# A two-layer trunk with eight experts on one core: the long-list path moved ahead, gate and up tiles side by side, the last group and the norm in a written order

## The chip, the core and the metric

One NeuronCore of a Trainium2 chip runs one program. It has TensorE (PE, matmuls, with its weight loads as PEld), VectorE (DVE), ScalarE (ACT), GpSimd (POOL) and SyncE (SP, which here issues nearly all DMAs). The metric is the device time of one execution in microseconds; "before" is the median of three runs, and one more execution was profiled.

## The reference

```python
for l in range(DEPTH):                      # 2 layers, 256 tokens, width 1024
    h = rms_norm(x, norm_mix[l])
    x = x + hybrid_mixer(h, ...)
    h = rms_norm(x, norm_ffn[l])
    if l % 2 == 0: x = x + swiglu(h, ...)       # dense, 3584 hidden units
    else:          x = x + moe_swiglu(h, ...)   # top 2 of 8 experts, 3584 hidden units each
return rms_norm(x, norm_final)

def swiglu(x, wg, wu, wd):
    return (jax.nn.silu(x @ wg) * (x @ wu)) @ wd
```

All weights are f32 in HBM, some 426 MB, of which the experts are 352 MB. Each is read once.

## The kernel before

The weights come as one stream of tiles of 128x2048 f32 (1 MB), in the order of use. An expert has 14 groups of 256 hidden units; a group has three tiles: gate (`ig`), up (`iu`) and down (`idn`). The eight experts are 112 groups, counted here from 0 to 111; the last expert has groups 98 to 111. I write idn(104) for the down tile of group 104.

A matmul takes f16. Each tile is therefore split into a high half, which ACT writes (the *head*, L113: scale and round), and a low half, which DVE writes (the *tail*, L117: what is left). Only the down tile of every odd group stays f32 and goes to PE whole (`whole`). So an even group has three tiles to split and an odd group two, 280 in all.

An expert works on the up to 80 tokens of its list (`CAP`). `gate_up(n)` is 96 matmuls (L287 to L289: high by high, high by low, low by high), first the gate tile's 48, then the up tile's 48; L289 is the one that needs the tail. Then ACT takes Silu of the gate half (L803), DVE multiplies by the up half (L807), and in even groups ACT and DVE split the product (L811, L812). `down(n)` adds the product with the down tile to two accumulators (L718 split, 12 matmuls; L712 whole, 8 instructions); it stands behind `gate_up(n+1)` on PE, so that the hidden step is covered. After the 14 groups of an expert the accumulators are copied (`evacuate`: L726, L727) and scattered back to the rows (`combine`: L736, L738).

In this stage the order on PE, DVE and ACT is the order in which the code is written (`manual_schedule`). `groups()` writes for each group n: gate_up(n), down(n-1), and then a loop of k heads and tails, with Silu behind the first head, the product behind the first tail, and L811 and L812 behind the second pair. k comes from `lead`, the number of tiles that shall be split ahead: it falls from 7 to 3 over the 112 groups. Loads go through SP; a tile's buffer is one of eleven, and SP issues a load when a buffer is free and the eighth load before it has landed.

Behind the last `gate_up` and before the last `down` stands a path for lists longer than 80 tokens (L837): if a count exceeds 80, a loop computes the rest with all tokens. With these inputs no list is that long, and each engine only branches past it. Behind it stand the last down, the last combine, the final norm (squares on ACT with a sum per half row, L930; sums, root and reciprocal per block of 128 rows, L931 to L934; scaling, L938 to L945) and four output DMAs (L946). That part is ordered by the scheduler.

Of the kernel before, what the change touches and what calls it, by code (L numbers as in the profile page):

```python
# [14 lines left out]
P = 128  # L15
T = 256
# [22 lines left out]
LEAD = (7.0, 3.0)  # L39

# [15 lines left out]
def trunk(ctx: ExitStack, tc: tile.TileContext, x, w, small, gates, last, out):  # L56
# [62 lines left out]
    def split_tile(i, r):  # L119

        t = spl.tile([P, 2, 2048], F16, name="hl")
# [301 lines left out]
    def gate_up(ig, iu, h, n, between=None):  # L423
# [80 lines left out]
    def moe(l, accs, extra_load):  # L504
# [226 lines left out]
        def combine(e, ye, c=None):  # L731
            for c in range(2) if c is None else (c,):
                for q in range(2):
                    o = mm((P, half))
                    for part in range(2):
                        PE.matmul(o, sgt[e][:, c * P:(c + 1) * P], ye[:, part, q * half:(q + 1) * half],  # L736
                                  start=(part == 0), stop=(part == 1))
                    V.scalar_tensor_tensor(yts(c, q), o.rearrange("p (n t) -> p n t", n=2), comb[:, c, e:e + 1],  # L738
                                           yts(c, q), op0=OP.mult, op1=OP.add)
# [31 lines left out]
        def groups():  # L771
            ready = None
            for n, (e, g) in enumerate(steps):
# [20 lines left out]
                lead = LEAD[0] + (LEAD[1] - LEAD[0]) * n / (len(steps) - 1)  # L794
                k = max(1 if n == 0 else 0, used + int(lead) - todo["n"])
# [3 lines left out]
                for j in range(k + 2):  # L799
# [29 lines left out]
            return before  # L829

        counts = {}
        with tc.manual_schedule(engines={mybir.EngineType.PE, mybir.EngineType.DVE, mybir.EngineType.Activation}):
            routing()
            before = groups()
        longest = counts["longest"]

        with tc.If(longest > CAP):  # L837
# [11 lines left out]
            hh = lambda part, k: h[:, part, k]  # L849
            for e in range(NE):  # L850
# [158 lines left out]
```

## Time and profile before

| | us |
|---|---|
| median of three runs | 1252.37 (1252.36 to 1254.17) |
| the profiled execution | 1254.29 |
| its span, first to last instruction | 1252.5 |
| PE busy | 1170.6 (93%) |
| DVE busy | 995.7 (79%) |
| ACT busy | 825.3 (66%) |

[...] The loads moved 343 GB/s over the whole span and about 419 GB/s over its second half, up to the last 40 us. A row of the timeline names start, duration, engine, line, operation and count, and in brackets how long the engine had been idle and what released it.

### The profile page before, as it was taken

How to read it: one execution, taken by the hardware profiler on the slowest of the kernel's cores; microseconds unless marked ns; L12 is line 12 of the kernel's file. 1: busy time of each engine (PE TensorE's matmuls, PEld its weight loads, DVE VectorE, ACT ScalarE, POOL GpSimd, SP SyncE). 2: the span in 40 equal slices, each digit the busy share in tenths (PEclk: the TensorE clock that was granted, in tenths of full speed). 3: DMA queues.
4: the chain of work that ended last, by engine and by line, in shares of the span. 5: the costliest groups of instructions: out<-in, count | busy, mean ns of one | idle time of the engine just before them, and what ended most of it. 6: DMA issues, size and time to landing. Idle time of an engine off the chain costs nothing. (4 is left out here: it accounts for less than half of the span.)

```text
span 1252.5 us, 34703 instructions
## 1 busy us (share of the span) xinstructions
PE 1170.6 (93%) x15707; PEld 902.4 (72%) x15707; DVE 995.7 (79%) x915; ACT 825.3 (66%) x814; POOL 0.8 (0%) x7
## 2 busy tenths in 40 slices
PE   6999999999999989999999898998989899899985
PEld 5887888888888766776676666766657676666663
DVE  7798666666888787998888797888789788779875
ACT  6965444444685686777767676766666676766764
POOL 0000000000000000000000000000000000000000
PEclk9999999999999999999999999999989999999998
DMA  9976555555547789999999999999999999999991
GB/s 360 420 292 241 203 202 202 202 203 202 194 161 285 265 312 396 420 420 419 418 420 419 420 419 420 419 419 419 419 420 417 419 419 417 420 418 413 419 366 69
DMA packets 61358, 431.84 MB, mean 345 GB/s; under 512 B 6928, under 2 KB 7056, under 8 KB 10000
## 3 DMA queue, kind: packets, MB, share of 16 engines
q1 hardware_dynamic: 61200, 429.52, 85.3%
q8 instruction: 125, 2.05, 0.7%
q14 instruction: 33, 0.27, 0.1%
HBM read 428.44 MB, written 1.05 MB: 343 GB/s over the span
## 5 line engine op out<-in xcount | busy, mean ns | idle before, releaser
L117 DVE SCALAR_TENSOR_TENSOR hl<-raw,hl 128x2048 f16<-128x2048 f32 x269 | 611.0, 2281 | 123.5 <-ACT hl L113 122.0
L113 ACT ACTIVATE hl<-raw 128x2048 f16<-128x2048 f32 x269 | 508.9, 1901 | 158.4 <-DMA raw<-in_w 156.6
L288 PEld LDWEIGHTS <-hl 128*128 128x128 f16 x4704 | 468.2, 100 | 39.2 <-issue 19.7
L289 PEld LDWEIGHTS <-hl 128*128 128x128 f16 x4704 | 467.6, 99 | 39.3 <-DVE hl L117 20.5
L287 PEld LDWEIGHTS <-hl 128*128 128x128 f16 x4704 | 468.1, 100 | 36.5 <-issue 14.9
L289 PE MATMUL mm<-he,hl 128*128 128x80 f16 x3584 | 398.6, 202 | 16.3 <-DVE hl L117 16.0
L287 PE MATMUL mm<-he,hl 128*128 128x80 f16 x3584 | 399.1, 202 | 0.0
L288 PE MATMUL mm<-he,hl 128*128 128x80 f16 x3584 | 399.0, 202 | 0.0
L125 DVE SCALAR_TENSOR_TENSOR hl<-raw,hl 128x2048 f16<-128x2048 f32 (+1 forms) x78 | 176.0, 2260 | 72.1 <-ACT hl L124 71.9
L287 PE MATMUL mm<-h,hl 128*128 128x256 f16 x768 | 209.0, 273 | 3.0 <-ACT h L237 2.8
L288 PE MATMUL mm<-h,hl 128*128 128x256 f16 x768 | 209.5, 273 | 1.8 <-DVE h L238 1.6
L289 PE MATMUL mm<-h,hl 128*128 128x256 f16 x768 | 209.5, 273 | 1.6 <-DVE hl L125 1.6
L712 PE MATMUL acc<-raw,hdm 128*80 128x512 f32 x448 | 210.3, 614 | 0.0
L124 ACT ACTIVATE hl<-raw 128x2048 f16<-128x2048 f32 (+1 forms) x78 | 146.1, 1881 | 93.3 <-PE mm L289 86.2
L718 PE MATMUL acc<-hl,hdm 128*80 128x512 f16 x672 | 161.9, 389 | 12.2 <-DVE hdm L812 9.5
L712 PEld LDWEIGHTS acc<-raw,hdm 128*80 128x80 f32 x448 | 65.6, 155 | 100.6 <-issue 99.2
L718 PEld LDWEIGHTS <-hdm 128*80 128x80 f16 x672 | 75.8, 120 | 76.8 <-DVE hdm L812 15.2
L803 ACT ACTIVATE sg<-mm 128x160 f32<-128x160 f32 x112 | 32.9, 294 | 46.9 <-PE mm L289 46.3
L288 PE MATMUL acc<-hd,hl 128*128 128x256 f16 x224 | 60.9, 273 | 0.2 <-DVE hd L462 0.2
L289 PE MATMUL acc<-hd,hl 128*128 128x256 f16 x224 | 60.9, 273 | 0.0
L287 PE MATMUL acc<-hd,hl 128*128 128x256 f16 x224 | 60.6, 273 | 0.0
L811 ACT ACTIVATE hdm<-sg 128x160 f16<-128x160 f32 x56 | 18.6, 333 | 35.1 <-DVE sg L807 32.7
(227 smaller groups left out, 606.1 us busy)
## 6 DMA issues: line engine op xcount, KB each, us to landing
raw<-in_w SPq DMA_DIRECT2D x400, 1024.0 KB, 19.7
raw<-in_w SPq DMA_DIRECT2D x6, 512.0 KB, 15.4
xT<-in_x SPq DMA_DIRECT2D x4, 256.0 KB, 3.9
gw<-in_gates SPq DMA_DIRECT2D x2, 512.0 KB, 9.9
gw<-in_w SPq DMA_DIRECT2D x1, 512.0 KB, 6.7
r<-in_w SPq DMA_DIRECT2D x1, 512.0 KB, 3.5
ig<-in_w SPq DMA_DIRECT2D x1, 512.0 KB, 5.6
a<-in_w SPq DMA_DIRECT2D x1, 512.0 KB, 6.5
```

Source lines behind the costliest of these rows:

```text
L113: S.activation(hi, src, AF.Copy, scale=SW)
L117: V.scalar_tensor_tensor(lo, src, SW, hi, op0=OP.mult, op1=OP.subtract)
L124: S.activation(hi, src, AF.Copy, scale=SW)
L125: V.scalar_tensor_tensor(lo, src, SW, hi, op0=OP.mult, op1=OP.subtract)
L287: PE.matmul(o, wt[0][:, cols], a_hi, start=start, stop=False, skip_group_check=True)
L288: PE.matmul(o, wt[0][:, cols], a_lo, start=False, stop=False, skip_group_check=True)
L289: PE.matmul(o, wt[1][:, cols], a_hi, start=False, stop=stop, skip_group_check=True)
L712: PE.matmul(eaccs[e][q], hd[:, c], wt[c][:, q * half:(q + 1) * half], start=(g == 0 and c == 0), stop=(g == NG - 1 and c == 1), skip_group ...
L718: PE.matmul(eaccs[e][q], hd[:, part, c], wt[wpart][:, c * D + q * half:c * D + (q + 1) * half], start=(g == 0 and c == 0 and part == 0 and ...
L803: S.activation(sg, bank[:, 0], AF.Silu, scale=IN_SCALE)
L811: S.activation(hd[:, 0], hf, AF.Copy)
```

## The change

- The path for long lists now stands eight groups ahead of the end (`REST`): `groups` runs to group 103, then comes the path, then groups 104 to 110, then `last_group`. The path loads its tiles through POOL into other buffers, and its tiles share the `hl` tag.
- `CLOSE` caps the lead at 2 in the last twelve groups and at 1 in the last four; behind the hidden step of each group a new loop splits up to three tiles ahead (one in group 110).
- The experts' gate and up weights are laid side by side (`sided`): the first tile of a group holds gate and up of its first 128 units, the second those of the other 128. `gate_up` takes the first tile's products for both, then the second's.
- `last_group` writes the last group out: its two tiles are split in halves, down(110) stands between the two halves of gate_up(111), the hidden step runs per 128 units, and the last down, the last combine and the norm follow in a written order on all three engines.

```diff
+CLOSE = ((12, 2.0), (4, 1.0))
+REST = 8
...
-        n = 2 if i in (0, NT - 2, NT - 1) else 1
+        n = 2 if i in (0, NT - 3, NT - 2, NT - 1) else 1
...
-        for a in range(2):
+        sided = not (isinstance(iu, int) and iu < MOE)
+        for t in range(2):
             for k in range(KD):
-                for c in range(2):
-                    mm3(o[a][c], wts[a], slice(k * 256 + c * P, k * 256 + (c + 1) * P), h(0, k), h(1, k),
+                for n in range(2):
+                    a, c = (n, t) if sided else (t, n)
+                    mm3(o[a][c], wts[t], slice(k * 256 + n * P, k * 256 + (n + 1) * P), h(0, k), h(1, k),
                         start=(k == 0 and (a, c) in first), stop=(k == KD - 1))
-            if a == 0 and between is not None:
-                between()
+            if t == 0 and between is not None:
+                between(*banks)
...
-        def groups():
-            ready = None
-            for n, (e, g) in enumerate(steps):
+        def groups(begin, end):
+            ready, before = later["ready"], later.get("before")
+            for n, (e, g) in list(enumerate(steps))[begin:end]:
...
                 lead = LEAD[0] + (LEAD[1] - LEAD[0]) * n / (len(steps) - 1)
+                lead = min([lead] + [x for at, x in CLOSE if n >= len(steps) - at])
...
+                for j in range(used + (1 if n == len(steps) - 2 else 3) - todo["n"]):
+                    next_heads()
+                    next_tails()
...
+        def last_group():
...
+            def unit(bank, c):
+                S.activation(sg[:, c], bank[:, 0, c], AF.Silu, scale=IN_SCALE)
+                V.scalar_tensor_tensor(hd[:, c], bank[:, 1, c], IN_SCALE * SY * SW, sg[:, c], op0=OP.mult, op1=OP.mult)
+            def between(bank):
+                down(*later["before"])
+                for n, piece in enumerate(pieces[iu]):
+                    head(piece)
+                    tail(piece)
+                unit(bank, 0)
+            for piece in pieces[ig]:
+                head(piece)
+                tail(piece)
+            bank = gate_up(ig, iu, lambda part, k: he[:, k, part], CAP, between)[0]
+            unit(bank, 1)
+            ready = B("ready", 1)
+            S.activation(ready, onesf, AF.Sqrt)
...
+            def square(c, q):
+                junk = t4(("a", "th")[q], (P, half))
+                S.activation(two(junk), yts(c, q), AF.Square, accum_out=fs[:, c, q:q + 1])
+            def rms(c):
+                V.scalar_tensor_tensor(fr[:, c:c + 1], fs[:, c, 1:2], 1.0 / D, pre[:, c:c + 1], op0=OP.mult, op1=OP.add)
+                S.activation(fr[:, c:c + 1], fr[:, c:c + 1], AF.Sqrt)
...
+            for c in range(2):
+                for q in range(2):
+                    add_up(e, ye, c, q)
+                    square(c, q)
+                    if q == 0:
+                        if c == 1:
+                            rms(0)
+                        V.tensor_scalar(pre[:, c:c + 1], fs[:, c, 0:1], 1.0 / D, EPS, op0=OP.mult, op1=OP.add)
+            scaled(0, 0)
+            V.reciprocal(fr[:, 0:1], fr[:, 0:1])
+            scaled(0, 1)
+            put(0)
+            rms(1)
+            scaled(1, 0)
+            V.reciprocal(fr[:, 1:2], fr[:, 1:2])
+            scaled(1, 1)
+            put(1)
...
             routing()
-            before = groups()
+            groups(0, len(steps) - REST)
...
-                            r = rawp.tile([P, 2048], F32, name="raw")
...
-                            nc.sync.dma_start(r, w[bass.ds(at, 1)].rearrange("o p c -> (o p) c"))
-                            split_tile(("spill", n), [(slice(0, 2048), r)])
+                            r = [(slice(j * 1024, (j + 1) * 1024), t4(t, (P, 1024))) for j, t in enumerate(SPARE[0])]
+                            for sl, t in r:
+                                G.dma_start(t, w[bass.ds(at, 1)].rearrange("o p c -> (o p) c")[:, sl])
+                            split_tile(("spill", n), r, spill[n])
...
-        ready = B("ready", 1)
-        S.activation(ready, xT[:, 0, 0:1], AF.Square)
-        S.activation(ready, ready, AF.Sqrt)
-        down(*before)
-        combine(NE - 1, evacuate(NE - 1))
+        with tc.manual_schedule(engines=ordered):
+            groups(len(steps) - REST, len(steps) - 1)
+            last_group()
```

ACT's instructions behind the hidden step of group 103, before: the heads (L113) of the tiles of group 104, then Silu (L803) and product copy (L811) of group 104, Silu of 105 and Silu of 106 among the heads of the next tiles.

```order
L113 ACTIVATE hl<-raw 128x2048 x3
L803 ACTIVATE sg_18341<-mm 128x160
L113 ACTIVATE hl<-raw 128x2048
L811 ACTIVATE hdm<-sg_18342 128x160
L113 ACTIVATE hl<-raw 128x2048
L803 ACTIVATE sg_18467<-mm 128x160
L113 ACTIVATE hl<-raw 128x2048 x3
L803 ACTIVATE sg_18591<-mm 128x160
```

The same place in the change, from where the path (L937) ends; head is L117, Silu L814, copy L822.

```order
L937 UNCONDITIONAL_BRANCH
L117 ACTIVATE hl<-raw 128x2048
L814 ACTIVATE sg_19968<-mm 128x160
L822 ACTIVATE hdm<-sg_19969 128x160
L117 ACTIVATE hl<-raw 128x2048 x2
L814 ACTIVATE sg_20094<-mm 128x160
L117 ACTIVATE hl<-raw 128x2048 x3
L814 ACTIVATE sg_20219<-mm 128x160
```

In the even group 104 the copy moved ahead of the second head; in the odd group 105 the order is the same. Groups 100, 102 and 106 read alike; in 108 both heads stand behind the copy.

DVE at the change's passage of the path: tails are L121, the product L818.

```order
L818 SCALAR_TENSOR_TENSOR hdm<-mm,sg_18218 128x160
L121 SCALAR_TENSOR_TENSOR hl<-raw,hl 128x2048
L937 COMPARE_AND_BRANCH
L939 TENSOR_SCALAR over<-slot 128x16
L940 TENSOR_TENSOR over<-over,comb 128x16
L952 TENSOR_LOAD each
```

The branch now stands behind the tail of the second tile of group 104, where before it stood behind the first `ye` of the last expert.

DVE from the last copy of `ye` on, before: four add-ups (L738), then the norm.

```order
L727 SCALAR_TENSOR_TENSOR ye<-acc,ye 80x512
L738 SCALAR_TENSOR_TENSOR xT<-mm,comb,xT 128x2x256 x4
L931 TENSOR_TENSOR fr<-fs 128x1
L938 TENSOR_TENSOR uc<-xT,cs 128x512
L932 TENSOR_SCALAR fr<-fr 128x1
L938 TENSOR_TENSOR uc<-xT,cs 128x512
L934 RECIPROCAL fr<-fr 128x1
```

The same in the change: add-ups are L742, `pre` is L919.

```order
L733 SCALAR_TENSOR_TENSOR ye<-acc,ye 80x512 x2
L742 SCALAR_TENSOR_TENSOR xT<-mm,comb,xT 128x2x256
L919 TENSOR_SCALAR pre<-fs 128x1
L742 SCALAR_TENSOR_TENSOR xT<-mm,comb,xT 128x2x256 x2
L896 SCALAR_TENSOR_TENSOR fr<-fs,pre 128x1
L919 TENSOR_SCALAR pre<-fs 128x1
L742 SCALAR_TENSOR_TENSOR xT<-mm,comb,xT 128x2x256
L910 TENSOR_TENSOR uc<-xT,cs 128x512
L921 RECIPROCAL fr<-fr 128x1
```

`pre` and the first block's sum, which need ACT's squares, now stand between the add-ups.

## Rows read from the trace of the kernel before

**Rows 1.** The page: a costly group (line, form, count, busy, idle), and DMA issues.
```profile
L113 ACT ACTIVATE hl<-raw 128x2048 f16<-128x2048 f32 x269 | 508.9, 1901 | 158.4 <-DMA raw<-in_w 156.6
...
raw<-in_w SPq DMA_DIRECT2D x400, 1024.0 KB, 19.7
```

**Rows 2.** Timeline of ACT: start, duration, what, idle time before and releaser.
```profile
1174.58 1.91 ACT L113 ACTIVATE hl<-raw 128x2048 f16<-128x2048 f32 x1 [0.55 <-DMA raw<-in_w]
...
1190.99 1.91 ACT L113 ACTIVATE hl<-raw 128x2048 f16<-128x2048 f32 x1 [2.08 <-DMA raw<-in_w]
...
1208.35 1.91 ACT L113 ACTIVATE hl<-raw 128x2048 f16<-128x2048 f32 x1 [0.58 <-DMA raw<-in_w]
1210.17 0.28 ACT L803 ACTIVATE sg<-mm 128x160 f32<-128x160 f32 x1
1210.82 1.91 ACT L113 ACTIVATE hl<-raw 128x2048 f16<-128x2048 f32 x1 [0.37 <-DMA raw<-in_w]
1212.86 0.34 ACT L811 ACTIVATE hdm<-sg 128x160 f16<-128x160 f32 x1
```

**Rows 3.** Timeline of DVE, the same stretch.
```profile
1210.29 2.29 DVE L117 SCALAR_TENSOR_TENSOR hl<-raw,hl 128x2048 f16<-128x2048 f32 x1 [0.20 <-ACT hl L113]
1212.50 0.32 DVE L807 SCALAR_TENSOR_TENSOR sg<-mm,sg 128x160 f32<-128x160 f32 x1
1212.76 2.29 DVE L117 SCALAR_TENSOR_TENSOR hl<-raw,hl 128x2048 f16<-128x2048 f32 x1
```

**Rows 4.** Timeline of PE: matmuls that waited for a tail.
```profile
1124.32 0.21 PE L289 MATMUL mm<-he,hl 128*128 128x80 f16 x1 [1.94 <-DVE hl L117]
...
1215.11 0.21 PE L289 MATMUL mm<-he,hl 128*128 128x80 f16 x1 [0.35 <-DVE hl L117]
...
1222.48 0.21 PE L289 MATMUL mm<-he,hl 128*128 128x80 f16 x1 [0.56 <-DVE hl L117]
```

**Rows 5.** Stretches: length, PE, PEld, DVE, ACT, POOL busy, granted clock, DMA, GB/s.
```profile
1222.50:1237.20 14.70, 14.70 (x170) 8.76 (x170) 7.80 (x8) 5.29 (x8) 0.00 (x0) 1.00 0.14 54
1205.00:1222.50 17.50, 15.38 (x261) 11.36 (x262) 14.66 (x11) 12.42 (x10) 0.00 (x0) 1.00 0.79 315
1126.00:1127.00 1.00, 1.00 (x11) 0.76 (x10) 0.06 (x1) 1.00 (x2) 0.00 (x0) 0.50 1.02 426
1128.00:1129.00 1.00, 1.00 (x4) 0.44 (x3) 1.00 (x1) 1.00 (x1) 0.00 (x0) 0.55 0.94 385
```

**Rows 6.** Line 837, the path: queue, operation, count, ns, first and last start.
```profile
L837 SPq EVENT_SEMAPHORE  x9: 17/17/17, 1217.8 to 1228.3; - x9
...
L837 ACTq EVENT_SEMAPHORE  x2: 17/17/17, 1239.5 to 1239.6; - x2
...
L837 SPq COMPARE_BRANCH  x1: 45/45/45, 1213.7 to 1213.7; - x1
...
L837 ACTq COMPARE_BRANCH  x1: 50/50/50, 1236.4 to 1236.4; - x1
```

**Rows 7.** Timeline of all engines from the last down on.
```profile
1233.64 3.60 PE L712 MATMUL acc<-raw,hdm 128*80 128x512 f32 x8
...
1240.29 0.57 ACT L726 ACTIVATE ye<-acc 80x512 f16<-80x512 f32 x1
1240.29 2.76 PE L736 MATMUL mm<-ye,sgt 80*128 80x512 f16 x8 [3.05 <-DVEq L837]
...
1241.50 0.74 DVE L738 SCALAR_TENSOR_TENSOR xT<-mm,comb,xT 128x512 f32<-128x512 f32 x1
...
1242.28 0.62 ACT L930 ACTIVATE a<-xT 128x512 f32<-128x512 f32 x1
1242.66 2.07 DVE L738 SCALAR_TENSOR_TENSOR xT<-mm,comb,xT 128x512 f32<-128x512 f32 x3 [0.42 <-PE mm L736]
1242.81 0.19 ACT L930 ACTIVATION_READ_ACCUMULATOR a<-xT 128x1 f32 x1
...
1247.96 0.72 ACT L943 ACTIVATE ge<-ge,fr 128x512 f32<-128x512 f32 x1 [0.47 <-DVE fr L934]
```

More of the change, by code (lines that the diff above doesn't have):

```diff
@@ L729, in evacuate, with add_up, combine @@
             return ye
[L731 to L739, printed above, removed]
+        def add_up(e, ye, c, q):
+            o = mm((P, half))
+            for part in range(2):
+                PE.matmul(o, sgt[e][:, c * P:(c + 1) * P], ye[:, part, q * half:(q + 1) * half],
+                          start=(part == 0), stop=(part == 1))
+            V.scalar_tensor_tensor(yts(c, q), o.rearrange("p (n t) -> p n t", n=2), comb[:, c, e:e + 1],
+                                   yts(c, q), op0=OP.mult, op1=OP.add)
+        def combine(e, ye, c):
+            for q in range(2):
+                add_up(e, ye, c, q)
         todo = {"heads": MOE + 10, "tails": MOE + 10, "n": 9}
@@ L828, in groups, with put, scaled @@
                 before = (e, g, idn, hd)
-            return before
+            later["ready"], later["before"] = ready, before
+        def last_group():
+            e, g = steps[-1]
+            ig, iu, idn = take(3)
+            he = hes[e]
+            pieces = {}
+            for i in (ig, iu):
+                t = spl.tile([P, 2, 2048], F16, name="hl")
+                pieces[i] = list(split_pieces(raw.pop(i), t))
+                parts[i] = [t[:, 0], t[:, 1]]
+            parts[idn] = [t[:, k:k + D] for _, t in raw.pop(idn) for k in range(0, t.shape[1], D)]
+            hd = wk.tile([P, 2, CAP], F32, name="hdl", tag="xs", bufs=2)
+            sg = wk.tile([P, 2, CAP], F32, name="sg0", tag="ssq")
+            def unit(bank, c):
[14 more added lines that the diff above has]
+            S.activation(ready, onesf, AF.Sqrt)
+            wt = parts.pop(idn)
+            for c in range(2):
+                for q in range(2):
+                    PE.matmul(eaccs[e][q], hd[:, c], wt[c][:, q * half:(q + 1) * half], start=False, stop=(c == 1),
+                              skip_group_check=True)
+            ye = evacuate(e)
+            gl = late["gl"]
+            fs, pre = B("fs", 2, 2), B("pre", 2)
+            fr = B("fr", 2)
+            two = lambda t: t.rearrange("p (n t) -> p n t", n=2)
+            ots = [t4(("uc", "ge")[c], (P, D)) for c in range(2)]
+            def square(c, q):
[4 more added lines that the diff above has]
+                S.activation(fr[:, c:c + 1], fr[:, c:c + 1], AF.Sqrt)
+            def put(c):
+                for q in range(2):
+                    sl = slice(q * half, (q + 1) * half)
+                    if q == 0:
+                        S.activation(ots[c][:, sl], ots[c][:, sl], AF.Copy, scale=fr[:, c:c + 1])
+                    else:
+                        V.tensor_scalar(ots[c][:, sl], ots[c][:, sl], fr[:, c:c + 1], None, op0=OP.mult)
+                    nc.sync.dma_start(out[c * P:(c + 1) * P, sl], ots[c][:, sl])
+            def scaled(c, q):
+                sl = slice(q * half, (q + 1) * half)
+                V.tensor_tensor(two(ots[c][:, sl]), yts(c, q), two(gl[:, sl]), op=OP.mult)
+            for c in range(2):
+                for q in range(2):
+                    add_up(e, ye, c, q)
+                    square(c, q)
+                    if q == 0:
+                        if c == 1:
[10 more added lines that the diff above has]
+            put(1)
@@ L831, in moe @@
         counts = {}
-        with tc.manual_schedule(engines={mybir.EngineType.PE, mybir.EngineType.DVE, mybir.EngineType.Activation}):
+        ordered = {mybir.EngineType.PE, mybir.EngineType.DVE, mybir.EngineType.Activation}
+        with tc.manual_schedule(engines=ordered):
             routing()
-            before = groups()
+            groups(0, len(steps) - REST)
         longest = counts["longest"]
@@ L849, in moe @@
             hh = lambda part, k: h[:, part, k]
+            spill = [spl.tile([P, 2, 2048], F16, name="spill", tag="hl") for _ in range(3)]
             for e in range(NE):
@@ L918, in trunk @@
     gw[1] = gate_weights(1)
[L919 removed]
+    accs = ffn(0, h, sums, lambda *_: finish1(), later1)
     h, sums, finish = residual(accs, nm[:, 8:16])
     accs = mixer(1, h, sums, finish, lambda sd: None)
[L922 to L946 removed]
+    moe(1, accs, gl_load)
 def _stream(np, inputs):
```

45 lines of the change are left out of this document (12 added, 33 removed).

## The prediction

> **What bounds the kernel now.** I read the timeline of ScalarE (ACT), VectorE (DVE) and TensorE (PE) over the last ten groups first, then PE's busy share by stretch, then the rows of the path for long lists, then the closing timeline.
>
> [rows 1]: ACT's heads (the f16 high halves, 1.9 us each) make ACT wait 158.4 us over the run, 156.6 of it for a transfer: the experts' stage runs at the pace of the loads. [rows 2] show that pace near the end: heads that wait for their tile begin 2.47 us apart (1208.35, 1210.82). [rows 3]: DVE's tail (the low half) starts when its head ends and takes 2.29 us, so a tile is usable some 4.2 us after landing. [rows 4]: PE waits 0.35 to 0.56 us in the middle of gate_up for the tail of the up tile. For groups 108 and 109 that is a loop with little to spare: PE is busy 15.38 of 17.5 us [rows 5].
>
> From 1222.5 us on PE has no gap until 1237.2 [rows 5]: half of gate_up(110), down(109), gate_up(111), down(110), down(111). So the end of down(111), which I call E (1237.2 before), is set by when gate_up(110) gets the tail of its second tile, and anything that makes PE late there reaches the end one for one. Behind E stand the path's branch and the norm: span end 1252.5, so E + 15.3.
>
> **The branch leaves the end: gain.** In [rows 7] PE begins the combine at 1240.29 after 3.05 us of waiting for DVE's passage of the path, and the second copy of `ye` starts on ACT at the same time. Without the branch that copy begins as soon as its matmuls end, about E; the first add-up follows 1.21 us behind it as in the rows (1240.29, 1241.50), so at E + 1.25 and not E + 4.26. Gain 3.0 us.
>
> **The branch at group 104: loss.** [rows 6]: ACT's compare-and-branch is issued at 1236.4 and its next instruction runs at 1239.5, 3.1 us later; SP's takes 4.1 us (1213.7 to 1217.8) with loads still in flight. In the change the ACT branch stands behind the head of idn(104), which began at 1174.58 in the trace [rows 2]. PE's first instruction after the path waits for ACT and DVE, so gate_up(104) starts at 1174.6 + 1.1 (how late that head starts in the new order, below) + 3.1 to 4.1, about 1179 to 1180; PE is free for it at about 1176. PE's spare time until the end takes most of this back. Laid out row by row with the durations of [rows 2 to 4], 0.8 us (branch of 3.1) to 1.8 us (4.1) is left at E. I take 1.8, since SP's row is the one taken with loads in flight. PE's idle time there is 2.9 to 3.9 us. [...]
>
> The SP queue has some 20 loads behind the branch. A load lands 19.7 us after its issue [rows 1], eight tiles deep, so a pause of 4.1 us leaves the queues filled: nothing. The end of the path holds SP until its own DMA semaphores have landed (up to 1228.3 in [rows 6], where nothing stood behind it); the change moves the path's loads to POOL, and SP's row in its order keeps no such wait. If that were wrong, a pause of 14.6 us (1213.7 to 1228.3) would cost several us.
>
> [...]
>
> **The order in the last twelve groups: loss.** CLOSE does not shorten what is split ahead: the new loop behind the hidden step brings the splits back to three tiles ahead in the same group. What it changes is which instruction stands first. In every even group (100 to 108) ACT before ran head(gate of n+1), Silu, head(up of n+1), then the copy L811; now the copy (L822) stands ahead of head(up). That copy waits for DVE's L818, and L818 stands behind the tail of gate(n+1). In the rows of group 108: head at 1208.35, landing of the up tile and its head at 1210.82, tail until 1212.58, L807 until 1212.82, copy at 1212.86 [rows 2, 3]. In the new order the head of the up tile starts after the copy, at 1213.2 and not 1210.82; its tail runs 1215.1 to 1217.4 and not to 1215.05; PE's wait in the middle of gate_up(109) grows from 0.35 to 2.6 us, or to 2.2 where PE itself comes later. So +2.3 us for the odd group.
>
> It then passes into the even group: Silu(109) waits for gate_up(109) and stands ahead of head(up 110). With gate_up(109) done at 1219.2, that head begins at 1219.6 and not at its landing, 1218.2 (three tiles of 2.47 behind 1210.82); +1.3 us. PE's spare time takes back about as much as comes on, not all of it. Continuing the same steps (each op at the latest of its landing, its input and the op ahead in its queue) the second half of gate_up is late by 2.2, 1.1, 2.9, 1.8, 3.5, 2.4 us in groups 101 to 106, and, behind a pause of the loads that moved all landings from 1190.99 on by 1.4 us [rows 2], by 2.7, 1.7, 3.3, 2.2 in 107 to 110. For before the same timetable gives E within 0.2 us of the trace. Loss at E +2.2; bounds 0, if PE's slack took all of it, and +4.
>
> **Last group, side by side.** The same 96 matmuls and the same down; down(110) moves between the halves, and the half of the hidden units waits under the first half of down(111). PE has no gap to close there, so the order gains nothing: +0.1. The matmuls of all other groups are the same in number and form; only columns change place in the tile.
>
> **The norm.** Before, four add-ups ran one behind the other on DVE, 0.67 us apart, and the sums came last. Now `pre` stands on DVE behind the first add-up and waits for ACT's square of it: 0.62 + 0.19 us with hand-overs [rows 7], 0.8 us of idle DVE. The same comes again behind the third add-up, where ACT still has the second's square ahead, and the sum of the first row block waits 0.2: +1.9 with the small steps. Against that the first block's sum and root no longer stand behind the last add-up (-0.5), and the 0.42 us that DVE waited for PE behind the first add-up goes with the branch (-0.4). From the first add-up to the end of the last scaling it was 7.2 us (1241.50 to 1247.96 + 0.72), now 8.2: +1.0, bounds -0.9 (all squares hidden) and +1.5.
>
> **Sum.** 1252.5 - 3.0 (branch out of the end) + 1.8 + 1.2 (branch at group 104, clock behind it) + 2.2 (order) + 0.1 (last group) + 1.0 (norm) = 1255.8 us of span; E = 1242.5, and 13.3 behind it. The profiled execution took 1254.29 with a span of 1252.5, and the median is 1252.37, 0.13 below that span. Forecast 1255.7 us, 0.27% above before.
>
> **Rivals.** *Faster.* PE's spare time, 12% of the stretch in [rows 5], swallows both the late up tiles and the branch before group 110, so E stays at 1237.2, and the squares are hidden: 1237.2 + 12.3 - 0.9 = 1248.6 of span, 1248.5 us; it stays under the border as long as the norm costs less than +0.5. It decides at the second half of gate_up(110): it must start by 1222.5, as in [rows 4]. For it: each group has some 1 us of PE waits to give. Against: ACT's own queue, not PE, carries the delay from group to group. 0.18.
>
> *No difference.* The branch costs the moved place next to nothing (3.1 us or less, and no fall of the clock): E = 1239.5 to 1240.3, span 1252.8 to 1253.6, 1252.7 to 1253.5 us. 0.28. [...]
>
> *Slower still.* [...] 0.14.
>
> [...]
>
> **How the numbers follow.** Forecast 0.40 (own range 1254.0 to 1257.2), no difference 0.28, slower still 0.14, faster 0.18. A measurement of this kernel tells about 0.2%, 2.5 us, from no change, so 1249.9 and 1254.9 are the borders: of the forecast's 0.40 some 0.28 lies above 1254.9. Slower 0.42, same 0.40, faster 0.18. The range leaves out two thirds of the faster case and the top of the slowest: 1249.4 to 1258.8.
>
> **What would show it.** ACT's L822 ahead of the second head in even groups, with that head some 2 us after its landing; PE waits of about 2 us for L121 in the middle of gate_up(101), (103), (107); a gap of 3 to 4 us at gate_up(104) with the clock at 0.50 after it; down(111) ending at 1241 to 1244; two waits of DVE's L919 of 0.8 us; from E to the end 13.3 us. The forecast is wrong if the up heads start at their landing, if E comes before 1239, or if E to the end is under 12.5.

## The result, and the profile after

The changed kernel took 1262.67 us (median of 6 runs, 1261.53 to 1263.56) beside 1252.96 for the kernel before on the same chip: 1.0076 of before, 95% interval 1.0066 to 1.0086, so 9.7 us slower. The forecast was 1255.7 in a range to 1258.8. The direction came out, the size did not. The profiled execution took 1263.56 us with a span of 1261.5 and is the one read here.

Executions differ in where the last twelve groups begin (down(99) ends at 1151.3 to 1156.2 us in the profiles that are read below). So I count from one fixed point: the end of down(99), the down ahead of the first reordered group. These are the rows of PE's timeline (start, duration, operation) for that down and for the last one, down(111), of the kernel after:

```profile
1149.68 3.60 PE L718 MATMUL acc<-raw,hdm 128*80 128x512 f32 x8
...
1244.58 3.63 PE L881 MATMUL acc<-raw,hdl 128*80 128x512 f32 x8
```

From 1153.28 to E = 1248.21 it is 94.9 us. In the kernel before, down(99) ended at 1153.72 (the row below) and E stood at 1237.24 [rows 7]: 83.5 us.

```profile
1150.12 3.60 PE L712 MATMUL acc<-raw,hdm 128*80 128x512 f32 x8
```

So 11.4 us were lost in twelve groups; the forecast had 5.3. Behind E it is 13.3 us to the end of the span, as forecast.

**The order.** The forecast had a copy on ACT ahead of the second head. ACT's timeline of group 102 after, then that of DVE (the idle time before each operation and its releaser in brackets):

```profile
1164.84 1.90 ACT L117 ACTIVATE hl<-raw 128x2048 f16<-128x2048 f32 x1
1167.38 0.30 ACT L814 ACTIVATE sg<-mm 128x160 f32<-128x160 f32 x1 [0.64 <-PE mm L293]
1170.14 0.34 ACT L822 ACTIVATE hdm<-sg 128x160 f16<-128x160 f32 x1 [2.46 <-DVE sg L818]
1170.38 1.89 ACT L117 ACTIVATE hl<-raw 128x2048 f16<-128x2048 f32 x1
```

```profile
1163.17 6.70 DVE L121 SCALAR_TENSOR_TENSOR hl<-raw,hl 128x2048 f16<-128x2048 f32 x3 [1.47 <-ACT hl L117]
1169.79 0.32 DVE L818 SCALAR_TENSOR_TENSOR sg<-mm,sg 128x160 f32<-128x160 f32 x1
1170.51 0.33 DVE L823 TENSOR_TENSOR hdm<-sg,hdm 128x160 f16<-128x160 f32 x1 [0.40 <-ACT hdm L822]
```

ACT stands still for 2.46 us with a landed tile in front of it: the head starts at 1170.38 without having waited for a transfer. In [rows 2] the second head waited for its DMA and the copy came behind it. PE then waits in the odd groups; its timeline at gate_up(101), (103), (104), (107) and (109):

```profile
1157.84 0.21 PE L293 MATMUL mm<-he,hl 128*128 128x80 f16 x1 [2.08 <-DVE hl L121]
...
1174.66 0.21 PE L293 MATMUL mm<-he,hl 128*128 128x80 f16 x1 [1.96 <-DVE hl L121]
...
1185.15 0.20 PE L291 MATMUL mm<-he,hl 128*128 128x80 f16 x1 [4.45 <-DVEq L937]
...
1211.11 0.21 PE L293 MATMUL mm<-he,hl 128*128 128x80 f16 x1 [2.05 <-DVE hl L121]
...
1224.59 0.21 PE L293 MATMUL mm<-he,hl 128*128 128x80 f16 x1 [1.71 <-DVE hl L121]
```

The same places in [rows 4] show 0.35 to 0.56 us near the end. And the clock, by stretch (length, then busy time of PE, PEld, DVE, ACT, POOL, granted clock as a share of full speed, DMA share, GB/s):

```profile
1159.00:1160.00 1.00, 1.00 (x19) 1.00 (x17) 0.99 (x1) 0.00 (x0) 0.00 (x0) 0.50 1.09 442
1176.00:1177.00 1.00, 1.00 (x19) 1.00 (x17) 0.80 (x1) 0.00 (x0) 0.00 (x0) 0.50 1.06 434
1187.00:1188.00 1.00, 1.00 (x19) 1.00 (x17) 1.00 (x2) 0.00 (x0) 0.00 (x0) 0.50 0.58 229
1211.00:1213.00 2.00, 1.89 (x48) 1.79 (x49) 2.00 (x2) 0.00 (x0) 0.00 (x0) 1.00 1.02 422
```

The clock fell to 0.50 behind the waits of 2.08 and 1.96 us and behind the path; behind the wait of 2.05 us at 1211 it stayed at 1.00.

**The branch.** The rows of line 937, the path (queue, operation, count, ns, first and last start):

```profile
L937 SPq EVENT_SEMAPHORE  x1: 17/17/17, 1163.3 to 1163.3; - x1
...
L937 SPq COMPARE_BRANCH  x1: 45/45/45, 1158.2 to 1158.2; - x1
L937 PEldq COMPARE_BRANCH  x1: 6129/6129/6129, 1176.7 to 1176.7; - x1
L937 ACTq COMPARE_BRANCH  x1: 50/50/50, 1177.4 to 1177.4; - x1
L937 DVEq COMPARE_BRANCH  x1: 72/72/72, 1179.5 to 1179.5; - x1
```

SP goes on 5.1 us after its branch; on ACT the next semaphore row is at 1183.0, 5.6 us behind the branch, on DVE at 1185.0, 5.5 us behind. In [rows 6] it was 3.1 us on ACT, with the loads done, and 4.1 on SP. Beside these three branches the transfers moved 382 to 414 GB/s; in [rows 6] it was 11 GB/s beside ACT's and 293 beside SP's. The price is higher where the transfers are, but no run changes them alone. The transfers slow for some time (229 GB/s at 1187), but that is not what was paid for: with the branch E is 84.7 us behind down(99) in old_order, without it 84.2 in old_order_no_path.

**The norm.** DVE's timeline behind E, with two waits for squares as forecast:

```profile
1249.49 0.74 DVE L742 SCALAR_TENSOR_TENSOR xT<-mm,comb,xT 128x512 f32<-128x512 f32 x1
1251.01 0.15 DVE L919 TENSOR_SCALAR pre<-fs 128x1 f32<-128x1 f32 x1 [0.79 <-ACT a L893]
...
1253.33 0.15 DVE L919 TENSOR_SCALAR pre<-fs 128x1 f32<-128x1 f32 x1 [0.56 <-ACT a L893]
...
1257.30 0.49 DVE L905 TENSOR_SCALAR ge<-ge,fr 128x512 f32<-128x512 f32 x1
```

From the first add-up to the end of the last scaling it is 8.3 us (1249.49 to 1257.79), forecast 8.2; before it was 7.2 in [rows 7].

### The profile page after: what moved, and what is told of

Read it like the earlier page. It is cut to its first block, busy times and chain, and to the rows that moved or that the text cites. A ratio compares the mean times of both kernels' runs of the same rounds, so it can differ in the third digit from the quotient of the medians.

```text
span 1261.5 us, 34708 instructions
## 1 busy us (share of the span) xinstructions
PE 1175.9 (93%) x15707; PEld 907.0 (72%) x15707; DVE 997.0 (79%) x917; ACT 823.3 (65%) x815; POOL 0.8 (0%) x7
## 5 line engine op out<-in xcount | busy, mean ns | idle before, releaser
L121 DVE SCALAR_TENSOR_TENSOR hl<-raw,hl 128x2048 f16<-128x2048 f32 x266 | 605.1, 2289 | 129.3 <-ACT hl L117 128.4
L117 ACT ACTIVATE hl<-raw 128x2048 f16<-128x2048 f32 x266 | 503.4, 1906 | 142.8 <-DMA raw<-in_w 139.9
L128 ACT ACTIVATE hl<-raw 128x2048 f16<-128x2048 f32 (+1 forms) x78 | 146.1, 1880 | 93.1 <-PE mm L293 86.2
L718 PE MATMUL acc<-raw,hdm 128*80 128x512 f32 x440 | 205.8, 612 | 0.0
L724 PE MATMUL acc<-hl,hdm 128*80 128x512 f16 x672 | 164.4, 394 | 11.4 <-DVE hdm L823 9.8
L814 ACT ACTIVATE sg<-mm 128x160 f32<-128x160 f32 x111 | 32.7, 294 | 67.2 <-PE mm L293 67.0
L822 ACT ACTIVATE hdm<-sg 128x160 f16<-128x160 f32 x56 | 18.6, 332 | 40.5 <-DVE sg L818 39.0
```

The lines of the kernel that those rows point to most:

```text
L117: S.activation(hi, src, AF.Copy, scale=SW)
L121: V.scalar_tensor_tensor(lo, src, SW, hi, op0=OP.mult, op1=OP.subtract)
L128: S.activation(hi, src, AF.Copy, scale=SW)
L718: PE.matmul(eaccs[e][q], hd[:, c], wt[c][:, q * half:(q + 1) * half], start=(g == 0 and c == 0), stop=(g == NG - 1 and c == 1), skip_group ...
L724: PE.matmul(eaccs[e][q], hd[:, part, c], wt[wpart][:, c * D + q * half:c * D + (q + 1) * half], start=(g == 0 and c == 0 and part == 0 and ...
L814: S.activation(sg, bank[:, 0], AF.Silu, scale=IN_SCALE)
```

## The experiments

"Behind down(99)" is the time from the end of down(99) to E in the one profile of each kernel; medians and ratios go by the runs beside the kernel before. "No path" means that the code for long lists is left out, which these inputs don't enter. All in one table:

| kernel | median us | ratio to before, 95% | E behind down(99) |
|---|---|---|---|
| before | 1252.4 to 1253.7 | 1 | 83.5 |
| changed | 1262.67 | 1.0076 (1.0066 to 1.0086) | 94.9 |
| old_order: path at 104 | 1253.65 | 1.0005 (0.9996 to 1.0014) | 84.7 |
| no_path: new order | 1258.61 | 1.0043 (1.0030 to 1.0056) | 91.9 |
| old_order_no_path | 1251.54 | 0.9991 (0.9982 to 1.0000) | 84.2 |
| order_alone | 1261.22 | 1.0072 (1.0056 to 1.0089) | 92.2 |
| copy_dve, no path | 1251.05 | 0.9984 (0.9974 to 0.9993) | 83.7 |
| copy_dve_path, path at 104 | 1254.69 | 1.0007 (0.9994 to 1.0019) | 86.2 |
| one_pair: group 100, no path | 1251.78 | 0.9990 (0.9981 to 0.9999) | 83.9 |
| late_pair: group 108, no path | 1254.33 | 1.0008 (0.9999 to 1.0017) | 86.4 |
| filler, no path | 1260.49 | 1.0058 (1.0044 to 1.0072) | 89.8 |
| filler2, no path | 1259.75 | 1.0047 (1.0033 to 1.0062) | 88.6 |
| path_early: new order, path at 84 | 1257.63 | 1.0035 (1.0023 to 1.0047) | 91.6 |
| norm_old | 1261.19 | 1.0055 (1.0038 to 1.0071) | not read |
| best1: old order, path at 84, old norm | 1249.81 | 0.9970 (0.9959 to 0.9982) | 83.4 |
| best2: the same, new norm | 1249.55 | 0.9968 (0.9956 to 0.9981) | 84.2 |

### Order and branch, each with and without the other

```diff
# old_order
-CLOSE = ((12, 2.0), (4, 1.0))
+CLOSE = ((2, 1.0),)
...
-                for j in range(used + (1 if n == len(steps) - 2 else 3) - todo["n"]):
-                    next_heads()
-                    next_tails()
# no_path
-        with tc.If(longest > CAP):
...
# order_alone (on the kernel before)
+CLOSE = ((12, 2.0), (4, 1.0))
...
+                lead = min([lead] + [x for at, x in CLOSE if n >= len(steps) - at])
...
+                for j in range(used + 3 - todo["n"]):
+                    next_heads()
+                    next_tails()
```

> The changed kernel with the old order in its last twelve groups (the copy of the hidden step stands behind the second head again); the path's branch stays at group 104, the last group and the norm stay as changed. First theory (the two losses feed each other: the copy ahead of the head takes the slack away, so the 5.5 us branch is never given back): the branch still stops the engines 4 to 5.5 us at group 104, but PE catches up before group 110, the end of down(111) comes at 1237.4 to 1239 and the time is 1251 to 1252.5, 0.992 of the changed kernel, about 0.999 of before. Second theory (the branch alone is the loss, in whichever order): the end of down(111) stays at 1244 or later, time 1258 to 1261. Third theory (the pause of the load queue starves the loads): the last tiles land late in this kernel too, time 1258 or more.

> The changed kernel without the code of the path for long lists, which these inputs don't enter: it leaves out the branch at group 104, all else is as changed. First theory: the order of the last twelve groups costs by itself 3 to 5 us at the end of down(111), which comes at 1240 to 1242, and the time is 1253 to 1255.5, 1.001 to 1.003 of before. Second theory (the branch is the whole loss): the end of down(111) at 1237.2 to 1238, time 1250.5 to 1251.5. Third theory: as the second, with the landings of the last loads back at 1226.3.

> The changed kernel with the old order in its last twelve groups and without the code of the path for long lists (not entered by these inputs). What is left of the change is the last group's halves and the written norm. All theories: the end of down(111) at 1237.2 to 1237.6 and 13.3 us behind it, time 1250.4 to 1251, 0.998 of before. It is the base from which the two parts of the change are counted: if order and branch only add, the cost of the order here plus the cost of the branch here is the loss of the changed kernel; the first theory has the loss of both together 3 us or more above that sum.

> The kernel before with the new order of the last twelve groups alone: the copy of the hidden step ahead of the second head in even groups from 100 on, the path for long lists where it was, the old last group and the old norm. First theory: up heads some 2.3 us late in groups 101, 103, 105, 107 and 109, PE waits of about 2 us there with the granted clock at 0.50 behind some of them, the end of down(111) at 1241 to 1243.5, time 1256 to 1258.5, 1.003 to 1.005 of before. Second theory: PE's slack takes it, the end of down(111) at 1237.2 to 1238, time 1252.4 to 1253.2.

Measured: the order costs 7.1 us by medians without the path (1258.61 against 1251.54) and 7.6 in the profiles; put alone into the kernel before, 8.2. My own first theory had given it 3 to 5, and the second theory (the branch alone) falls with it. The branch costs 2.1 us in the old order (1253.65 against 1251.54; 0.5 in the profiles) and 4.1 in the new (1262.67 against 1258.61; 3.1); 1253.65 and 1251.54 lie 1.2 and 0.5 us above what was expected of them. So the two parts seem to feed each other, by 2.0 us (2.6 in the profiles), not by the "3 us or more" I had expected. An amount of this size the intervals of the medians alone don't tell from none; that most of the loss is the order's own they do show. The third theory, starved loads, falls too: old_order keeps the branch and with it SP's pause, and its E is 84.7 behind down(99).

What the branch does in the old order is seen on PE's timeline of old_order. It waits longer than in the changed kernel and still gives nearly all of it back:

```profile
1180.53 0.23 PE L291 MATMUL mm<-he,hl 128*128 128x80 f16 x1 [6.09 <-ACTq L934]
...
1235.11 3.63 PE L878 MATMUL acc<-raw,hdl 128*80 128x512 f32 x8
```

And the new order without the branch, no_path, on PE and ACT:

```profile
1189.03 0.25 PE L293 MATMUL mm<-he,hl 128*128 128x80 f16 x1 [2.05 <-DVE hl L121]
...
1205.99 0.21 PE L293 MATMUL mm<-he,hl 128*128 128x80 f16 x1 [2.06 <-DVE hl L121]
```

```profile
1192.37 0.30 ACT L814 ACTIVATE sg<-mm 128x160 f32<-128x160 f32 x1 [3.93 <-PE mm L293]
1192.57 5.50 ACT L117 ACTIVATE hl<-raw 128x2048 f16<-128x2048 f32 x3
1198.71 0.30 ACT L814 ACTIVATE sg<-mm 128x160 f32<-128x160 f32 x1 [0.64 <-PE mm L293]
1201.47 0.34 ACT L822 ACTIVATE hdm<-sg 128x160 f16<-128x160 f32 x1 [2.46 <-DVE sg L818]
1201.71 3.69 ACT L117 ACTIVATE hl<-raw 128x2048 f16<-128x2048 f32 x2
1209.27 0.30 ACT L814 ACTIVATE sg<-mm 128x160 f32<-128x160 f32 x1 [3.87 <-PE mm L293]
```

DVE's timeline of the same stretch:

```profile
1194.50 6.70 DVE L121 SCALAR_TENSOR_TENSOR hl<-raw,hl 128x2048 f16<-128x2048 f32 x3 [1.47 <-ACT hl L117]
1201.12 0.32 DVE L818 SCALAR_TENSOR_TENSOR sg<-mm,sg 128x160 f32<-128x160 f32 x1
...
1203.64 4.49 DVE L121 SCALAR_TENSOR_TENSOR hl<-raw,hl 128x2048 f16<-128x2048 f32 x2 [1.48 <-ACT hl L117]
```

Here is the ring that I had not drawn as one. It starts and ends where an odd gate_up ends on PE, so a turn is a pair of groups:

- gate_up(105) ends, and ACT starts its Silu at 1192.37.
- Three heads follow on ACT one behind the other (1192.57), without waiting for a transfer, and three tails on DVE (1194.50 to 1201.20).
- The product of group 106 stands behind the third tail (1201.12), the copy behind the product (1201.47), the next head behind the copy (1201.71), its tail behind that head (1203.64).
- The second half of gate_up(107) starts behind that tail (1205.99), and at its end Silu comes again, at 1209.27.

This is 16.9 us, however long the tiles have been lying there; the pair takes the same by PE's waits (1189.03 to 1205.99, 17.0 us). The loads, six tiles 2.47 us apart as in [rows 2], would need 14.8. Each pair falls further behind, and nothing is there to take it back. The expectation of copy_dve below gives a turn 7.3 us, from the end of gate_up(106) to 1205.99. That is not a turn: Silu(106), begun at 1198.71, is done 2.1 us before the product, which waits for the third tail.

### The copy off the ring, one pair alone, the path elsewhere

```diff
# copy_dve (on no_path)
-                        S.activation(hd[:, 0], hf, AF.Copy)
+                        if n >= len(steps) - 12:
+                            V.tensor_copy(hd[:, 0], hf)
+                        else:
+                            S.activation(hd[:, 0], hf, AF.Copy)
# one_pair (on old_order_no_path; late_pair: 108)
+ONE = (100,)
...
+                lead = min(lead, 2.0) if n in ONE else lead
...
+                for j in range(used + 3 - todo["n"] if n in ONE else 0):
+                    next_heads()
+                    next_tails()
# path_early
-REST = 8
+REST = 28
```

> The changed kernel without the code of the path for long lists (not entered by these inputs), in the new order, with one operation on another engine: in the last twelve groups the copy of the hidden step runs on DVE and not on ACT, so nothing on ACT waits for DVE between the Silu and the second head. Ring theory (Silu, DVE product, copy on ACT, head, tail, then the second half of the next gate_up: a ring that starts at the end of gate_up and takes some 7.3 us wherever the loads stand): the PE waits of 2 us in the odd groups fall to 0.6 us, no granted clock of 0.50 from group 101 on, the end of down(111) returns from 91.9 us behind that of down(99) to 84 to 86, time 1251.3 to 1253. Rival (the later splits of CLOSE cost, not the copy): waits of 2 us remain, time 1257 to 1259.

> Without the code of the path (not entered by these inputs), the old order in the last twelve groups except in group 100, where the copy stands ahead of the second head. Ring theory: one PE wait of 2.0 to 2.1 us in gate_up(101), with a granted clock of 0.50 behind it some 3.5 us lost; in the old order PE has 0.5 us of waits in each half group to give, so it is made good by group 108 and the end of down(111) is 84.2 to 85.5 us behind that of down(99), time 1251.5 to 1252.5. Rival (lost time is never given back, each wait counts whole): 86.5 to 88 us, time 1254 to 1255.5.

> Without the code of the path (not entered by these inputs), the old order in the last twelve groups except in group 108, where the copy stands ahead of the second head: the same one late head as in the run with group 100, eight groups later. If what decides is the PE waiting time left before the end: the wait in gate_up(109) grows from 0.35 to about 2 us; only the waits of 0.4, 0.6 and 0.2 us of groups 110 and 111 are left to give, so the end of down(111) is 85 to 87.5 us behind that of down(99) (upper end with a fall of the clock), against 83.9 with the late head in group 100; time 1252 to 1254.5. If one late head costs the same in both places, or nothing: 83.5 to 84.5 us, time 1251 to 1252.

> The changed kernel with the path's branch ahead of group 84 and not of 104, in a stretch that still has the old order; the order of the last twelve groups is the new one. If stalls are given back in the old order and kept in the new one: 4 to 6 us of PE idle at group 84, made good by group 92, and the time is that of the kernel without the path, 1258.2 to 1259.5, some 4 us below the changed kernel. If the branch costs the same wherever it stands: 1262 to 1263.5. If the pause of the load queue is what costs: the loads are 4 us late from group 86 to the end, 1261 to 1264.

copy_dve settles what in the order costs. One operation of 0.25 us on another engine, all else in the new order, and the whole 7.6 us are gone: 1251.05, 83.7 behind down(99). The PE waits are 0.98 to 1.18 us and not the 0.6 I expected (the second head still starts later than in the old order), yet pairs follow the loads again. ACT's timeline in copy_dve shows it:

```profile
1193.31 1.91 ACT L117 ACTIVATE hl<-raw 128x2048 f16<-128x2048 f32 x1 [1.25 <-DMA raw<-in_w]
1195.13 0.29 ACT L814 ACTIVATE sg<-mm 128x160 f32<-128x160 f32 x1
1195.80 1.91 ACT L117 ACTIVATE hl<-raw 128x2048 f16<-128x2048 f32 x1 [0.39 <-DMA raw<-in_w]
1200.77 1.91 ACT L117 ACTIVATE hl<-raw 128x2048 f16<-128x2048 f32 x1 [3.06 <-DMA raw<-in_w]
```

Heads wait for DMA, as in [rows 2]. Over the whole run the heads of no_path waited 143.4 us for transfers, those of copy_dve 159.8, those of [rows 1] 156.6: where ACT waits less for its tiles here, it is because it is late.

one_pair and late_pair put the same wait of 2.08 us (at 1156.65 and 1216.21) with a fall of the clock behind it into one place each (0.50 and 0.81 in two stretches of 2 us from 1158 in one_pair, 0.64 and 0.51 from 1217 in late_pair). In group 101 it costs nothing at E (83.9 against 84.2 in old_order_no_path); in group 109 2.2 us (86.4 against the same 84.2; medians 1254.33 against 1251.78 in one_pair). So a stall is made good as long as PE has waits left to give (most of those in best2's last groups, which have the old order, are 0.36 to 0.60 us), and counts where there are none.

path_early is 5.0 us below the changed kernel and 1.0 below the one without the path: the branch at group 84, in the old order, costs nothing that can be seen in the medians; PE's wait for it there was 6.5 us in best2. (The profiled execution of path_early took 1261.78 us, 4.2 more than the median, so only its 91.6 is read from it.)

### The waits and the clock apart

```diff
# filler (on no_path), in groups 101 to 109, the odd ones
...
+                            PE.matmul(bank[:, j % 2, 1], wg[:, at:at + P], zeros, start=False, stop=False,
+                                      skip_group_check=True)
...
# filler2: in group 109 ahead of the first half
...
+        if ahead is not None:
+            ahead(banks[0])
...
```

> The changed kernel without the code of the path (not entered by these inputs), in the new order, with 48 matmuls on a tile of zeros, each 128x80, between the halves of gate_up in groups 101, 103, 105, 107 and 109: PE is busy for 1.9 us where it waited for 2.05 us. They add zero to the bank. It separates the wait from the clock. If the fall of the clock behind the waits is a part of the loss: the granted clock stays near 1.00 from 1150 us to the end, a pair of groups takes 15.6 to 15.8 us and not 17.0, and the end of down(111) comes 87 to 89 us behind that of down(99) and not 91.9; time 1254 to 1256. If the clock falls for another reason, or its fall costs nothing: 91 us or more, time 1258 or more.

> As the run with matmuls on zeros between the halves of gate_up (without the code of the path, new order), but in group 109, where the wait stands ahead of the first half, 42 of them ahead of that half and none between the halves. In the first such run the 48 of group 109 followed a wait of 1.71 us and added 1.9 us. If the clock's share of the order's loss is some 4 us: no granted clock of 0.50 from 1150 us to the end, the end of down(111) 87.5 to 88.5 us behind that of down(99), against 91.9 without the extra matmuls and 84.2 in the old order; time 1254.5 to 1259, by how late down(99) comes. If the extra matmuls cost as much as the clock: 90 to 92 us.

The stretch of the last groups, filler2 first, then no_path (columns as above):

```profile
1155.00:1243.00 88.00, 84.21 (x1412) 62.10 (x1411) 64.79 (x48) 54.26 (x49) 0.00 (x0) 1.00 0.81 324
```

```profile
1155.00:1243.00 88.00, 77.85 (x1127) 55.40 (x1126) 63.21 (x45) 51.92 (x47) 0.00 (x0) 0.94 0.76 306
```

ACT's Silu of groups 105 and 107 in filler2, one turn of the ring:

```profile
1193.91 0.30 ACT L835 ACTIVATE sg<-mm 128x160 f32<-128x160 f32 x1 [2.50 <-PE mm L295]
...
1209.44 0.30 ACT L835 ACTIVATE sg<-mm 128x160 f32<-128x160 f32 x1 [2.50 <-PE mm L295]
```

With PE kept busy the clock holds 1.00 over this stretch, where it was 0.94, and E is 88.6 behind down(99), not 91.9. So of the order's 7.6 us some 3.3 are the clock and 4.3 the waits themselves; a turn then takes 15.5 us and not 16.9, still over 14.8. The difference stands in one link: from the end of PE's wait in gate_up(107) to its Silu it is 3.3 us in no_path (1205.99 to 1209.27) and 1.9 in filler2 (1207.53 to 1209.44). In filler the 48 matmuls of group 109 stood behind the wait and added 1.2 us. The times of both missed what I expected (1254 to 1256 for filler, 1254.5 to 1259 for filler2): down(99) ended at 1156.1 to 1156.2 in both profiles, 3.5 us later than in no_path. Why the stretch ahead came later there, in a kernel changed only behind it but for a small tile of zeros, stays open. The shares rest on one profile each.

### What keeps the branch's stall

```diff
# copy_dve_path (on the changed kernel, with its path)
-                        S.activation(hd[:, 0], hf, AF.Copy)
+                        if n >= len(steps) - 12:
+                            V.tensor_copy(hd[:, 0], hf)
+                        else:
+                            S.activation(hd[:, 0], hf, AF.Copy)
```

> The changed kernel with its path at group 104 and its new order, the copy of the hidden step on DVE and not on ACT in the last twelve groups, nothing else. If it is the ring through ACT's copy that keeps the path's stall: the waits of 2 us are gone, the stall of 4.5 to 6 us at group 104 is given back but for 1 to 2.5 us as in the old order, the end of down(111) 84 to 86 us behind that of down(99), time 1252 to 1254. If the later splits of the new order keep the stall: 87 us or more, time 1255 or more.

A miss: 86.2 and 1254.69, 3.6 us over copy_dve. PE's wait at the branch was 5.35 us. So the ring through ACT's copy is not what keeps the stall in the new order; without it the branch still costs 2.5 us at E, against 0.5 in the old order and 3.1 with the ring. Where it is kept, the three pairs of kernels with and without the path show. How many us later gate_up of each group ends with the path (read at the start of the next down, from the end of down(99)):

| group | 104 | 105 | 106 | 107 | 108 | 109 | 110 |
|---|---|---|---|---|---|---|---|
| old_order, over old_order_no_path | 6.8 | 5.2 | 4.2 | 3.4 | 2.4 | 1.8 | 0.8 |
| changed, over no_path | 8.0 | 4.5 | 4.5 | 3.1 | 3.1 | 3.1 | 3.1 |
| copy_dve_path, over copy_dve | 6.4 | 4.8 | 4.3 | 3.1 | 2.6 | 2.5 | 2.5 |

Up to group 107 all three win back about alike. From 108 on the old order goes on and the new one all but stops, with the ring or without it. 108 is where the lead is capped at 1, and there all heads stand behind a Silu that waits for PE. ACT's timeline of copy_dve_path shows them, none with a wait for a transfer:

```profile
1210.92 0.30 ACT L814 ACTIVATE sg<-mm 128x160 f32<-128x160 f32 x1 [2.44 <-PE mm L293]
1211.12 5.50 ACT L117 ACTIVATE hl<-raw 128x2048 f16<-128x2048 f32 x3
1219.46 0.30 ACT L814 ACTIVATE sg<-mm 128x160 f32<-128x160 f32 x1 [2.84 <-PE mm L293]
1219.66 3.70 ACT L117 ACTIVATE hl<-raw 128x2048 f16<-128x2048 f32 x2
```

In copy_dve PE still waits 0.98 and 0.31 us in group 109 at the same places as in copy_dve_path, so these are not slack for a stall. That the cap of 1 keeps the rest is argued from these rows; a run with that cap alone was not made.

### The norm, and a version that beats both

```diff
# norm_old: sums behind all four add-ups
...
-                    if q == 0:
-                        if c == 1:
-                            rms(0)
-                        V.tensor_scalar(pre[:, c:c + 1], fs[:, c, 0:1], 1.0 / D, EPS, op0=OP.mult, op1=OP.add)
...
# best1 (the edits of norm_old and old_order)
...
-REST = 8
+REST = 28
# best2 (on best1), in place of the two scalings of q = 1
...
+                V.scalar_tensor_tensor(two(ots[c][:, sl]), yts(c, 1), fr[:, c:c + 1], two(gl[:, sl]), op0=OP.mult,
+                                       op1=OP.mult)
...
```

> The changed kernel with the four add-ups one behind the other on DVE and the sums behind them, as before. If the written order costs 1.0 us: from the end of down(111) to the end of the span 12.2 to 12.4 us and not 13.3, no wait of DVE for the squares between the add-ups, time about 1261.7. If the squares are covered in some other way: 13.3 us, time 1262.7.

> The changed kernel with the old order in the last twelve groups, the path's branch ahead of group 84, and the norm as before. By the parts: the end of down(111) 83.5 to 84.5 us behind that of down(99) and 12.3 us to the end; a stall of 6 us at group 84 that is made good; time 1250 to 1251, 0.998 of before. If the stall at group 84 is not made good: 1253 to 1256.

> As the kernel with the old order, the branch ahead of group 84 and the old norm, with a new order of the norm: the four add-ups one behind the other but for one small step whose square is long done, and the second half of each row block scaled by the root and by the weights in one DVE operation, not two. DVE then has 6.4 us of work from the first add-up to the last scaling and not 7.2. Expected 11.4 to 11.7 us from the end of down(111) to the end, time 1249.2 to 1250.3, 0.9975 of before. If DVE is not what sets it there: as with the old norm, 12.3 us and 1250 to 1251.

With the old norm it is 11.75 us from E to the end, in norm_old and in best1, and 13.25 in the changed kernel: the written norm costs 1.5 us beside an old one that has lost the branch. The medians of norm_old and the changed kernel differ by the same 1.5 us, which their intervals don't tell apart. (The profiled execution of norm_old took 1269.69 us, 8.5 more than its median; only the stretch behind E is read from it, and best1's profile has the same length there.) best1 is 3.7 us below before, 12.9 below the changed kernel. In best2 it is 6.0 us from the first add-up to the end of the last scaling (6.7 in best1). DVE's timeline of best2:

```profile
1238.78 2.05 DVE L742 SCALAR_TENSOR_TENSOR xT<-mm,comb,xT 128x512 f32<-128x512 f32 x3
1240.76 0.14 DVE L915 TENSOR_SCALAR pre<-fs 128x1 f32<-128x1 f32 x1
1240.82 0.74 DVE L742 SCALAR_TENSOR_TENSOR xT<-mm,comb,xT 128x512 f32<-128x512 f32 x1
...
1243.99 0.75 DVE L904 SCALAR_TENSOR_TENSOR ge<-xT,fr,cs 128x512 f32<-128x512 f32 x1
```

`pre` waits for nothing, one add-up later than in the change. From E to the end it is 11.3 us; the medians of best1 and best2 differ by 0.3 us, which their intervals don't tell apart.

## Why the prediction was right and wrong

**The branch leaves the end: right.** E to the end is 13.3 us as forecast, and the path no longer stands there.

**The branch at group 104 and the clock behind it, +3.0: right in sum for the new order, by luck.** 3.1 us at E in the profiles, 4.1 by medians. The parts were off: the branch took 5.1 to 5.6 us and not 4.1, with fuller transfers beside it (382 to 414 GB/s, and 293 beside SP's before), and PE's wait was 4.45 and not 2.9 to 3.9. PE fell 6.7 us behind no_path between gate_up(103) and gate_up(104), and 4.8 us of its whole lag were won back by 107; in the old order nearly all of it was. The clock fell to 0.50 behind the wait, as forecast. The sum's 1.2 us for it was my estimate, and no run shows that term by itself: the runs show 3.1 us at E for the branch and the clock together. SP did not wait for the path's transfers, also as forecast: its one semaphore row of the path is at 1163.3, 5.1 us behind its branch. The branch rows themselves last 45 to 72 ns on SP, ACT and DVE; but the next row of the queue comes 5.1 to 5.6 us later, and that is what the kernel pays.

**The order, +2.2: the step that failed.** It measured 7.6 at E. (Put alone into the kernel before, with its old last group, it was 8.6.) The rows that change place, the late head and the size of PE's waits (some 2 us forecast, 1.71 to 2.08 measured) were right. Wrong was the sentence "PE's spare time takes back about as much as comes on, not all of it". How many us later than in the kernel before gate_up of each group ends, read as above, beside the forecast's series (it is for the second half of gate_up):

| group | 101 | 102 | 103 | 104 | 105 | 106 | 107 | 108 | 109 | 110 |
|---|---|---|---|---|---|---|---|---|---|---|
| forecast | 2.2 | 1.1 | 2.9 | 1.8 | 3.5 | 2.4 | 2.7 | 1.7 | 3.3 | 2.2 |
| filler2, clock held | 2.3 | 2.3 | 4.4 | 4.1 | 5.8 | 4.7 | 4.9 | 3.9 | 5.7 | 4.8 |
| no_path | 2.8 | 3.3 | 4.9 | 4.6 | 7.7 | 6.7 | 8.2 | 7.2 | 9.0 | 8.1 |

With the clock held the first step and all steps from 105 on come out within 0.3 us; the timetable had the ring's links. But it let group 102 and group 104 each take back 1.1 us, as the landings near the end of [rows 2] allow, and they took back 0.0 and 0.3. In the kernel before, ACT's three heads behind Silu(101) already ran without waiting for a transfer:

```profile
1158.38 5.71 ACT L113 ACTIVATE hl<-raw 128x2048 f16<-128x2048 f32 x3
```

So there was no wait to give in group 102; what was lost in these first two pairs stayed. That is most of the 2.6 us between forecast and filler2. The other 3.3 us are the clock, which the sum had only once, behind the branch, and which [rows 4, 5] had shown behind a wait of this very size: 0.50 after 1.94 us.

**Last group, +0.1: right within what can be seen.** From the end of down(109) to the start of down(111) it is 5.87 us before and 6.10 after; the other kernels have 5.87 (copy_dve) to 6.50 (old_order_no_path).

**The norm, +1.0: right.** 8.3 against 7.2 us. The two waits of DVE were 0.79 and 0.56 us for a forecast of 0.8 twice. The 1.5 us of norm_old agree: the forecast had +1.9 - 0.5 for the order and -0.4 for a wait that goes with the branch.

In E's own terms: 83.5 + 0.7 (what old_order_no_path has more than before, nearly all of it in the last group) + 7.6 (order) + 0.5 (branch in the old order) + 2.6 (both together) = 94.9.

## What to carry to other kernels

Before a step is put ahead of another on an engine's queue, follow its inputs back around, and at each link ask which input comes last: if they return to the engine that will wait for the result, the delay is no longer one late tile but a ring whose length is a floor for every turn, whatever the loads do. Whether a group can take back a delay is read at that group: a head that waits for no transfer has nothing to give. A stall costs what the waits left behind it can't take back, so move it to where the most of them follow, and don't tighten the stretch behind it in the same change. Waits of PE of about 2 us are to be priced with the clock: it was 3.3 of the order's 7.6 us here.

## What was not expected of the hardware

The clock's answer to a wait of 2 us was not regular. It was 0.50 behind 1.96 and 2.08 us in the changed kernel and behind 2.05 us in no_path, and 0.58 and 0.52 over the stretches of 2 us behind 2.08 and 2.06 us there; it stayed at 1.00 behind 2.05 us in the changed kernel (at 1211) and behind 1.45 in no_path (at 1173.49). A branch past code that is not run cost PE 4.45 us of waiting in the changed kernel, with 382 to 414 GB/s of transfers beside the branches, 5.35 in copy_dve_path, 6.09 in old_order and 6.5 in best2, and 3.05 us in [rows 7], where the loads were done.
